# A hybrid encoder trunk: the 24 adaLN weight tiles of each layer move from the attention part to the branch part, into the ring of the weight stream

## The chip, the cores and the metric

The kernel runs on one core of a Trainium2 chip. The metric is device time of one execution in microseconds (us), the median of several runs. TensorE (PE) does the matmuls; VectorE (DVE), ScalarE (ACT) and GpSimd (POOL) do the rest; SyncE (SP) issues nearly all DMAs, in the order in which they are written.

## The reference, cut to what matters

Two requests of 256 tokens (512 columns in all) go through two layers of width 1024 with shared weights:

```python
mod = silu(c) @ w_mod + b_mod                    # (1024) x (1024, 6144), per request
sh1, sc1, gt1, sh2, sc2, gt2 = split(mod, 6)
h = rmsnorm(x) * (1 + sc1) + sh1
p = h @ w_in                                     # MLA, RG-LRU, DeltaNet inputs and three gates
o_mla, o_rg, o_gdn = mla(p), rglru(p), gdn(p)    # the three branches
m = sum_b sigmoid(gate_b) * (o_b @ w_branch[b])
x = x + gt1 * (m @ w_out)
h2 = rmsnorm(x) * (1 + sc2) + sh2
x = x + gt2 * convglu(h2)
```

In the RG-LRU each direction d has r = sigmoid(xb @ w_a + b_a), log_a = -8 * r * softplus(-lam), a = exp(log_a), and a factor sqrt(1 - exp(2 log_a)) on its input; then a scan over the tokens. The gated DeltaNet (GDN) has four heads, each a chain of small triangular solves and products.

## The kernel before, in words

Activations lie with channels on the 128 partitions and the 512 tokens on the free axis. Weights come as a stream of 128 x 128 units, eight to a chunk of 512 KB. `prefetch` (L375) loads a chunk into one of `NRAW = 3` buffers named `raw`, two chunks ahead of use; `split_chunk` (L382) splits it into a high part `wh` (ACT, L391) and a low part `wl` (DVE, L298), and each unit is then used by three matmuls of 512 columns (`mm3`).

The order of PE and SP is fixed by hand. `BRANCHES` (L33) lists the jobs of a layer: `in6` (first six input blocks), `uq`/`uk`/`uv` (up projections of MLA), `gate.b.d` and `br.b.d` (gate and branch product of branch b, output block d), `gq`/`gk`/`gv`/`z` (GDN), `x`/`g`/`b` (RG-LRU input, its gate, and the two products of one direction). Side work (attention, the GDN heads, the modulation) are generators that a `Driver` (L141) steps between the matmuls. The driver keeps a clock of its own, which adds an estimate for each matmul; a generator yields a wait of so many us (table `SLACK`) or an event, and is stepped when the clock has passed it. `drv.until(event)` steps what is due, and when nothing is, moves that clock ahead. The clock only decides where instructions stand in PE's and SP's order; on the chip an instruction waits for its data alone.

The modulation of a layer (`modulation`, L443, and `mod_gen`) multiplies silu(c) with tiles of w_mod: one tile of 512 KB is four products of fp32 (eight matmul instructions, `mod<-mraw,csil`). Here 24 tiles are in question, blocks 4 to 9, whose values (gt1, sh2, sc2) are first read in the output projection. Before the change they are spawned right after `in6` (L1091): pace 5.0 on the driver's clock, two buffers `mraw` of their own (`mla_raw`, L1051), each next load written behind the products of a tile. `close` (L1117), which frees MLA's memory, waits for `ev_mod`, their end. The job `uk.0` begins with `drv.until(ev_ckv)`, and `ev_ckv` is set to 152.5 us after the low-rank norm was written (`SLACK["low_rank_out"]`, set at L791), so all tiles that are left are written ahead of `uk.0`.

After `close`, the branch part runs until `close2`: GDN heads (`solve`, then `combine`, whose DMAs dl, Lb, dx and W go over SP), the RG-LRU, gates and branch products. Tiles of the RG-LRU and the gates share a tag `rt` with `RT = 8` buffers. In `rg_scan` the decay is scaled on DVE (L933) and then read by an exp and a tanh on ACT (L935, L936).

Of the kernel before, what the change touches and what calls it, by code (L numbers as in the profile page):

```python
# [8 lines left out]
F32 = mybir.dt.float32  # L9
# [3 lines left out]
AF = mybir.ActivationFunctionType  # L13
ALU = mybir.AluOpType
# [4 lines left out]
P = 128  # L19
# [7 lines left out]
UC = 8  # L27
# [5 lines left out]
BRANCHES = """  # L33
    in6 gate.0.0 uq.0 uq.1 gate.0.1 uq.2 uq.3 uq.4 uq.5 uk.0 uk.1 gq.0 uk.2 gk.0 uk.3 pad uv gv.0
    gate.0.2 gate.0.3 gate.0.4 gate.0.5 gate.0.6 gate.0.7 br.0.0 br.0.1 br.0.2 br.0.3 br.0.4 br.0.5
    br.0.6 br.0.7 close gq.1 gk.1 gv.1 x.0 x.1 b.0.0 g.0 b.0.1 g.1 b.1.0 x.2 b.1.1 g.2 x.3 b.2.0
    b.2.1 gq.2 gk.2 gv.2 g.3 b.3.0 b.3.1 gate.1.0 br.1.0 gate.1.1 br.1.1 gq.3 gate.1.2 gate.1.3
    br.1.2 z.0 gk.3 br.1.3 gate.2.0 gv.3 gate.2.1 gate.1.4 z.1 gate.2.2 gate.1.5 br.1.4 gate.1.6 z.2
    gate.1.7 gate.2.3 gate.2.4 gate.2.5 br.1.5 br.1.6 br.1.7 z.3 gate.2.6 mid gate.2.7 br.2.0 br.2.1
    br.2.2 br.2.3 br.2.4 br.2.5 br.2.6 br.2.7"""  # L40


def jobs():
# [17 lines left out]
SLACK = {  # L61
    "modev": 0.7, "att_s": 3.2, "att_t": 1.8, "att_e": 1.0, "low_rank": 11.8, "low_rank_out": 152.5, "mla": 0.2,
# [3 lines left out]
    "rg_all": 16.0, "ssq": 6.5, "kq": 8.0, "norm": 2.8, "normed": 17.0, "mod1": 5.0, "mod2": 8.0,  # L66
    "kd": 0.1, "start": 0.6, "diag2": 4.6, "cq": 2.1, "lr_diag": 5.3, "diag": 30.4}


# [165 lines left out]
def _body(es, tc, nc, xT, cT, wall, wmod, pvec, fng, cst, rope, xinit, yT, dbg):  # L235
    V, A, G = nc.vector, nc.scalar, nc.gpsimd
    drv = Driver()
# [4 lines left out]
    sp = es.enter_context(tc.tile_pool(name="small", bufs=1))  # L242
    xp = es.enter_context(tc.tile_pool(name="xm", bufs=8))
    hp = es.enter_context(tc.tile_pool(name="h", bufs=1))
    wp = es.enter_context(tc.tile_pool(name="w", bufs=2))
# [5 lines left out]

    def fill(pool, size):
        return pool.tile([P, size // 4], F32, name="fill", tag="fill", bufs=1)
    fill(sp, 160)


    cs = cp.tile([P, NCC], F32, name="cs")
# [42 lines left out]
    def stt(out, a, s, b, op0, op1):  # L300
        V.scalar_tensor_tensor(out, a, s, b, op0, op1)  # L301
# [11 lines left out]
    def aux_tile(shape=(P, T), name="aux"):  # L313
        return aux.tile(list(shape), F32, name=name, tag="aux")
# [51 lines left out]
    GS = (slice(0, S), slice(S, T), slice(0, T))  # L366


    NRAW = 3
    state = {"l": 0, "u": 0, "piece": None, "job": ""}  # L370

    loads, pieces = {}, {}
# [2 lines left out]
    def prefetch(at):  # L375
        if at not in loads:
            loads[at] = wp.tile([P, UC * P], F32, name="raw", tag="raw", bufs=NRAW)
            nc.sync.dma_start(loads[at], wall[at])
        return loads[at]
# [58 lines left out]
    def preload(l, blocks, tile_of):  # L438
        for i in range(4 * len(blocks)):
            loaded[l, 4 * blocks[0] + i] = tile_of(4 * blocks[0] + i)  # L440


    def modulation(l, groups, pace, tile_of, ahead):  # L443
        todo = [4 * g[0] + i for g in groups for i in range(4 * len(g))]

        def load():
            if todo:
                i = todo.pop(0)
                loaded[l, i] = tile_of(l, i)
        for _ in range(ahead):  # L450
            load()
        return mod_gen(l, groups, pace, load)
# [87 lines left out]
    def setup(l):  # L540
        def pcol(name):
            o, w = PV[name]
            return pv[:, l, o:o + w]
        d = {}
        t = sp.tile([P, 8], F32, name="p_sp", tag="p_sp", bufs=2)
        nl = sp.tile([P, 8], F32, name="p_nl", tag="p_nl", bufs=2)
        V.tensor_scalar(nl, pcol("rg_lam"), -1.0, None, ALU.mult)
        softplus(t, nl, 8)
        V.tensor_scalar(t, t, 4.0, None, ALU.mult)
        d["sp4"] = t  # L550
        t = sp.tile([P, 16], F32, name="p_hb", tag="p_hb", bufs=2)
        o, _ = PV["rg_b_a"]
        V.tensor_scalar(t, pv[:, l, o:o + 16], 0.5, None, ALU.mult)
        d["hb"] = t
        t = sp.tile([P, 1], F32, name="p_ng", tag="p_ng", bufs=2)
        V.tensor_scalar(t, pcol("gdn_norm_g"), 0.5, None, ALU.mult)
        d["ng"] = t
        t = sp.tile([P, 8], F32, name="p_ea", tag="p_ea", bufs=2)
        A.activation(t, pcol("a_log"), AF.Exp)
        V.tensor_scalar(t, t, -1.0, None, ALU.mult)  # L560
        d["nea"] = t
        prm[l] = d
# [100 lines left out]
    for k in range(8):  # L663
        t = xp.tile([P, T], F32, name="x", tag="x")
        nc.sync.dma_start(t, xT[:, k, :])
        xs.append(t)
    for b in range(4):
        preload(0, (b,), mraw)
        if b < NRAW:
            prefetch((0, b))  # L670
    later(stp)
    acc = stp.tile([P, T], F32, name="acc")
    for k in range(8):
        t = stp.tile([P, T], F32, name="sq", tag="t", bufs=4)
# [4 lines left out]
    ssq = aux_tile((P, 4), "ssq")  # L679
# [26 lines left out]
    for l in range(depth):  # L706
# [5 lines left out]
        pr = prm[l]  # L712
# [7 lines left out]
        mstack = ExitStack()  # L720
        mp = mstack.enter_context(tc.tile_pool(name="mla", bufs=1, side="right"))
        M2 = 10
        rstack = ExitStack()
        rp = rstack.enter_context(tc.tile_pool(name="mraw", bufs=1))
        gdn = GDN(nc, tc, locals())
        mixed = [None] * 8
        cq, ckv, o_mla = [], [], []
# [190 lines left out]
        def rg_scan(i, d):  # L918
            xc, xh, xl = xcs[i]
            if d == 0:  # L920
                drv.until(rev[i])
            zr = gemm([(xh, xl)])
            zi = gemm([(xh, xl)])
            c = d * 4 + i
            if d == 0:
                dirs.append(ap.tile([P, 2, T], F32, name="rs", tag="rs", bufs=RS))
            s = dirs[0][:, d, :]
            u = ap.tile([P, T], F32, name="ru", tag="rt", bufs=RT)
            a = ap.tile([P, T], F32, name="ra", tag="rt", bufs=RT)
            m = ap.tile([P, T], F32, name="rm", tag="rt", bufs=RT)  # L930
            A.activation(s, zr, AF.Tanh, bias=pr["hb"][:, c:c + 1], scale=0.5)
            A.activation(u, zi, AF.Tanh, bias=pr["hb"][:, 8 + c:9 + c], scale=0.5)
            V.tensor_scalar(s, s, 1.0, pr["sp4"][:, c:c + 1], ALU.add, ALU.mult)  # L933
            stt(u, u, 1.0, xc, ALU.add, ALU.mult)
            A.activation(a, s, AF.Exp, scale=-1.0)  # L935
            A.activation(s, s, AF.Tanh)  # L936
            A.activation(m, a, AF.Square)
            stt(s, m, 1.0, s, ALU.add, ALU.mult)
            f = 0 if d == 0 else S - 1
            V.memset(s[:, f::S], 1.0)  # L940
            V.memset(a[:, f::S], 0.0)
            dirs.append((u, a))
            if d == 0:
                return
            s2 = dirs.pop(0)
            A.activation(s2, s2, AF.Sqrt, bias=tiny, scale=0.0625)
            for d, (u, a) in enumerate(dirs):
                mul(u, u, s2[:, d, :])
                o = slice(None, None, -1 if d else 1)
                V.tensor_tensor_scan(s2[:, d, o], a[:, o], u[:, o], 0.0, ALU.mult, ALU.add)  # L950
            h0, h1 = s2[:, 0, :], s2[:, 1, :]
            dirs.clear()
            add(h0, h0, h1)
            mul(xc, h0, gls[i])
            debug(f"org{i}_{l}", xc)
            split(xc, xh, xl)
            o_rg.append((xh, xl))
            rev["all"] = drv.event()
            rev["all"].set(SLACK["rg_all"])
# [86 lines left out]
            uv.clear()  # L1046


        ev_mod = drv.event()

        def mla_raw(l, i):  # L1051
            raw = rp.tile([P, UC * P], F32, name="mraw", tag="mraw", bufs=2)
            nc.sync.dma_start(raw, wmod[l, i])
            return raw

        def beside(gen):
            yield from gen
            ev_mod.set(0.0)


        def next_raw(l, i):
# [13 lines left out]
        for job in JOBS:  # L1075
            k, *ix = job
            state["job"] = k
            if k == "in6":
# [9 lines left out]
                key_rope(misc)  # L1088
                ev_cq.set(SLACK["cq"])
                drv.spawn(low_rank())  # L1090
                drv.spawn(beside(modulation(l, ((4, 5, 6, 7), (8, 9)), SLACK["mod1"], mla_raw, 2)))  # L1091
            elif k in ("gq", "gk", "gv"):
                if k == "gq" and ix[0] >= 2:
                    drv.until(gdn.ev_free[ix[0] - 2])
# [22 lines left out]
            elif k == "close":  # L1117
                for t in range(8):
                    debug(f"K{t}_{l}", Kt[:, t, :])
                    debug(f"Q{t}_{l}", Qt[:, t, :])  # L1120
                drv.until(ev_mod)
                fill(mp, 1888)
                rstack.close()
                mstack.close()
                RT, RS = 8, 2
                ap = stack.enter_context(tc.tile_pool(name="rg", bufs=1))
                g2stack = ExitStack()
                gdn.g2 = g2stack.enter_context(tc.tile_pool(name="g2", bufs=1, side="right"))
                for hd in range(4):
                    drv.spawn(gdn.solve(hd))  # L1130
                gdn.xi = gdn.g2.tile([P, 8, 16], F32, name="xi", tag="xi")
                nc.sync.dma_start(gdn.xi, xinit)
            elif k == "x":
# [21 lines left out]
            elif k == "close2":  # L1155
                stack.close()
                rstack = ExitStack()
                rp = rstack.enter_context(tc.tile_pool(name="oraw", bufs=1))
# [11 lines left out]
            elif k == "out":  # L1170
                d, g = ix
# [23 lines left out]
            elif k == "down":  # L1195
                d, g = ix
# [7 lines left out]
                t = x1[d]  # L1204
                for e in ((0, 1) if g == 2 else (g,)):
                    c = GS[e]
# [536 lines left out]
```

## Time and profile before

| what | value |
|---|---|
| median of 3 runs | 2112.28 us (2110.99 to 2116.43) |
| profiled execution, its own time | 2115.39 us |
| its span, first to last instruction | 2113.6 us |
| PE busy | 1976.4 us, 94% |
| DVE / ACT / POOL busy | 1246.3 / 817.0 / 256.7 us |
| mean granted TensorE clock | 0.953 of 2.4 GHz |

Times in the profile are us from the first instruction. The engine named in front of an operation did it; "out<-in" names the tile written and the tile read; "[idle before <-releaser]" is the time that the engine stood idle ahead of it and what ended that.

### The profile page before, as it was taken

How to read it: one execution, taken by the hardware profiler on the slowest of the kernel's cores; microseconds unless marked ns; L12 is line 12 of the kernel's file. 1: busy time of each engine (PE TensorE's matmuls, PEld its weight loads, DVE VectorE, ACT ScalarE, POOL GpSimd, SP SyncE). 2: the span in 40 equal slices, each digit the busy share in tenths (PEclk: the TensorE clock that was granted, in tenths of full speed). 3: DMA queues.
4: the chain of work that ended last, by engine and by line, in shares of the span. 5: the costliest groups of instructions: out<-in, count | busy, mean ns of one | idle time of the engine just before them, and what ended most of it. 6: DMA issues, size and time to landing. Idle time of an engine off the chain costs nothing.

```text
span 2113.6 us, 29530 instructions
## 1 busy us (share of the span) xinstructions
PE 1976.4 (94%) x11563; PEld 1580.1 (75%) x11563; DVE 1246.3 (59%) x2338; ACT 817.0 (39%) x1275; POOL 256.7 (12%) x511
## 2 busy tenths in 40 slices
PE   9939998999999999999996699979999999999998
PEld 5717776788788788887874377768887878888887
DVE  5606578766366766653355175888553667666534
ACT  3404437533233444432242153565332335444322
POOL 1100036131300100000011000361421001000000
PEclk9959999999999999999998599989999999999999
DMA  8362132231426233353544412321322353232333
GB/s 299 134 202 67 55 92 64 68 83 52 111 86 214 80 100 93 97 179 110 191 126 140 161 60 72 90 65 51 96 72 78 115 185 93 97 100 92 99 99 110
DMA packets 141852, 231.45 MB, mean 110 GB/s; under 512 B 79760, under 2 KB 84240, under 8 KB 141712
## 3 DMA queue, kind: packets, MB, share of 16 engines
q1 hardware_dynamic: 136240, 221.95, 33.9%
q10 hardware_dynamic: 5472, 7.61, 1.1%
q8 instruction: 91, 1.49, 0.3%
q14 instruction: 49, 0.40, 0.1%
HBM read 221.66 MB, written 7.86 MB: 109 GB/s over the span
## 4 chain that ended last, share of the span: by engine, by line
PE 80%; DVE 7%; DMA 6%; ACT 2%; issue 2%; POOL 1%; SPq 1%; DVEq 0%; ACTq 0%; POOLq 0%
PE mm_up L220 23%; PE mm_down L220 11%; PE mm_gate L220 10%; PE mm_br L220 6%; DMA mraw<-in_wmod_dram 4%; PE mm_in L220 3%; PE mm_out L220 3%; PE mod L220 2%; PE mm_gk L220 2%; PE mm_gq L220 2%; PE mm_gv L220 2%; PE mm_g L220 1%; PE att_s L220 1%; PE gdn_rec L220 1%; PE mm_z L220 1%
## 5 line engine op out<-in xcount | busy, mean ns | idle before, releaser
L298 DVE TENSOR_TENSOR wl<-raw,wh 128x1024 fp32r<-128x1024 f32 x304 | 373.8, 1230 | 320.9 <-ACT wh L391 314.5
L391 ACT CAST wh<-raw 128x1024 fp32r<-128x1024 f32 x304 | 318.7, 1049 | 501.3 <-PE mm_down L220 130.5
L220 PE MATMUL mm_up<-hh,wh 128*128 128x512 f32 x704 | 275.6, 391 | 3.5 <-POOL hh L308 3.5
L220 PE MATMUL mm_up<-hl,wh 128*128 128x512 f32 x704 | 275.6, 391 | 0.0
L220 PE MATMUL mm_up<-hh,wl 128*128 128x512 f32 x704 | 275.1, 391 | 0.0
L301 DVE SCALAR_TENSOR_TENSOR cv<-mm_up,pv,cv 128x510 f32<-128x510 f32 x176 | 131.2, 748 | 61.3 <-ACT cv L569 58.0
L220 PE MATMUL mm_gate<-hh,wh 128*128 128x512 f32 x384 | 160.6, 418 | 0.0
L220 PEld LDWEIGHTS mm_up<-hh,wh 128*128 128x128 f32 x704 | 132.9, 189 | 31.7 <-POOL hh L308 3.9
L220 PEld LDWEIGHTS mm_up<-hl,wh 128*128 128x128 f32 x704 | 133.0, 189 | 27.9 <-DVE hl L298 0.4
L220 PEld LDWEIGHTS mm_up<-hh,wl 128*128 128x128 f32 x704 | 133.0, 189 | 27.5
L220 PE MATMUL mm_gate<-hl,wh 128*128 128x512 f32 x384 | 150.8, 393 | 0.0
L220 PE MATMUL mm_gate<-hh,wl 128*128 128x512 f32 x384 | 150.8, 393 | 0.0
L220 PE MATMUL mm_down<-ah,wh 128*128 128x512 f32 (+1 forms) x396 | 146.1, 369 | 0.0
L220 PE MATMUL mm_down<-ah,wl 128*128 128x512 f32 (+1 forms) x396 | 145.0, 366 | 0.6 <-DVE wl L298 0.6
L220 PE MATMUL mm_down<-al,wh 128*128 128x512 f32 (+1 forms) x396 | 144.9, 366 | 0.0
L220 PE MATMUL mod<-mraw,csil 128*32 128x256 f32 x512 | 56.3, 532 | 73.2 <-DMA mraw<-in_wmod_dram 73.0
L308 POOL TENSOR_SCALAR hh<-hn 128x256 fp32r<-128x256 f32 x64 | 34.0, 544 | 684.9 <-ACT hn L586 682.4
L569 ACT ACTIVATE cv<-mm_up,pv 128x512 f32<-128x512 f32 x88 | 68.5, 780 | 89.2 <-PE mm_up L220 89.2
L220 PEld LDWEIGHTS mod<-mraw,csil 128*32 128x32 f32 x512 | 12.3, 128 | 112.2 <-DMA mraw<-in_wmod_dram 102.3
L220 PEld LDWEIGHTS mm_down<-ah,wh 128*128 128x128 f32 x396 | 74.7, 189 | 15.0 <-issue 3.3
L220 PEld LDWEIGHTS mm_gate<-hh,wl 128*128 128x128 f32 x384 | 72.6, 189 | 16.0
L220 PEld LDWEIGHTS mm_down<-ah,wl 128*128 128x128 f32 x396 | 74.7, 189 | 13.0 <-DVE wl L298 0.8
(386 smaller groups left out, 3973.8 us busy)
## 6 DMA issues: line engine op xcount, KB each, us to landing
raw<-in_wall_dram SPq DMA_DIRECT2D x304, 512.0 KB, 3.6
mraw<-in_wmod_dram SPq DMA_DIRECT2D x64, 512.0 KB, 4.2
oraw<-in_wmod_dram SPq DMA_DIRECT2D x16, 512.0 KB, 7.1
hraw<-in_wmod_dram SPq DMA_DIRECT2D x32, 256.0 KB, 5.2
x<-in_xT_dram SPq DMA_DIRECT2D x8, 256.0 KB, 6.0
W<-dx SPq DMA_DIRECT2D x32, 64.0 KB, 2.3
xr<-in_xT_dram ACTq DMA_DIRECT2D x8, 256.0 KB, 3.3
xdram<-x ACTq DMA_DIRECT2D x16, 128.0 KB, 2.5
```

The source lines that it names most:

```text
L220: return self.pe.matmul(out, lhsT, rhs, **kw)
L298: (eng or V).tensor_tensor(out, a, b, ALU.subtract)
L301: V.scalar_tensor_tensor(out, a, s, b, op0, op1)
L308: G.tensor_scalar(hi, x, 1.0, 0.0, ALU.mult, ALU.add)
L391: A.copy(wh, raw)
L569: A.activation(dst, ps, AF.Identity, bias=bias, scale=w[lo])
```

## The change

The descriptor space of software DMAs is cut to 2 KB, which gives 14 KB per partition. They go to a fourth `raw` buffer (4 KB) and to `RT = 13`, five more `rt` tiles (10 KB). The two `mraw` buffers go; the 24 tiles of w_mod are spawned at `close`, at pace 8.0, one load ahead, from the ring of the `raw` buffers. Seven of the eight gates of branch 1 are written between the RG-LRU's products, ahead of `br.1.0`. The scale of the decay becomes scale and bias of the two ACT instructions.

```diff
-    gate.0.2 ... close gq.1 gk.1 gv.1 x.0 x.1 b.0.0 g.0 b.0.1 g.1 b.1.0 x.2 b.1.1 g.2 x.3 b.2.0
-    b.2.1 gq.2 gk.2 gv.2 g.3 b.3.0 b.3.1 gate.1.0 br.1.0 gate.1.1 br.1.1 gq.3 gate.1.2 gate.1.3
-    br.1.2 z.0 gk.3 br.1.3 gate.2.0 gv.3 gate.2.1 gate.1.4 z.1 gate.2.2 gate.1.5 br.1.4 gate.1.6 z.2
-    gate.1.7 gate.2.3 gate.2.4 gate.2.5 br.1.5 br.1.6 br.1.7 z.3 gate.2.6 mid gate.2.7 br.2.0 br.2.1
+    ... close gq.1 gk.1 gv.1 x.0 x.1 b.0.0 g.0 b.0.1 gate.1.0 g.1 b.1.0 x.2 b.1.1 gate.1.1
+    g.2 x.3 b.2.0 gate.1.2 b.2.1 gq.2 gk.2 gv.2 gate.1.3 g.3 b.3.0 gate.1.4 b.3.1 gate.1.5 gate.1.6
+    br.1.0 br.1.1 gq.3 br.1.2 z.0 gk.3 br.1.3 gate.2.0 gv.3 gate.2.1 br.1.4 z.1 gate.2.2 br.1.5
+    gate.1.7 z.2 br.1.6 gate.2.3 gate.2.4 br.1.7 gate.2.5 z.3 gate.2.6 mid gate.2.7 br.2.0 br.2.1
-    "mod1": 5.0
+    "mod1": 8.0
-    NRAW = 3
+    NRAW = 4
+        d["ns4"] = sp.tile([P, 8], F32, name="p_ns", tag="p_ns", bufs=2)
+        V.tensor_scalar(d["ns4"], t, -1.0, None, ALU.mult)
-            V.tensor_scalar(s, s, 1.0, pr["sp4"][:, c:c + 1], ALU.add, ALU.mult)
-            A.activation(a, s, AF.Exp, scale=-1.0)
-            A.activation(s, s, AF.Tanh)
+            p4, n4 = pr["sp4"][:, c:c + 1], pr["ns4"][:, c:c + 1]
+            A.activation(a, s, AF.Exp, bias=n4, scale=n4)
+            A.activation(s, s, AF.Tanh, bias=p4, scale=p4)
-        def mla_raw(l, i):
-            raw = rp.tile([P, UC * P], F32, name="mraw", tag="mraw", bufs=2)
+        def branch_raw(l, i):
+            raw = wp.tile([P, UC * P], F32, name="raw", tag="raw", bufs=NRAW)
             nc.sync.dma_start(raw, wmod[l, i])
-                drv.spawn(beside(modulation(l, ((4, 5, 6, 7), (8, 9)), SLACK["mod1"], mla_raw, 2)))
-                drv.until(ev_mod)
-                rstack.close()
-                RT, RS = 8, 2
+                RT, RS = 13, 2
+                drv.spawn(modulation(l, ((4, 5, 6, 7), (8, 9)), SLACK["mod1"], branch_raw, 1))
-    nc = _bacc.Bacc("TRN2", target_bir_lowering=False, num_devices=1)
+    nc = _bacc.Bacc("TRN2", target_bir_lowering=False, num_devices=1, dynamic_dma_scratch_size=2048)
```

## Rows read from the trace of the kernel before

**Rows 1.** Busy time by stretch; second row: layer 1; columns stand in the first line.
```profile
core 0: us, PE busy (x) PEld busy (x) DVE busy (x) ACT busy (x) POOL busy (x), PEclk, DMA share, GB/s
100.33:161.89 61.56, 24.09 (x178) 7.58 (x177) 3.89 (x11) 1.17 (x2) 0.00 (x0) 0.53 0.61 188
1140.60:1202.07 61.47, 24.22 (x178) 7.70 (x177) 3.89 (x11) 1.17 (x2) 0.00 (x0) 0.54 0.61 188
161.89:189.00 27.11, 26.43 (x110) 21.27 (x111) 14.40 (x21) 11.21 (x17) 0.00 (x0) 0.93 0.18 58
279.00:435.00 156.00, 141.29 (x1136) 115.08 (x1135) 130.62 (x255) 92.82 (x153) 59.67 (x111) 0.95 0.27 71
474.55:617.50 142.95, 139.09 (x1072) 115.35 (x1071) 71.19 (x134) 45.41 (x76) 26.13 (x64) 0.99 0.28 80
```

**Rows 2.** What PE waited for: us in total, times, longest.
```profile
PE mod L220 <- DMA mraw<-in_wmod_dram: 73.0, 32, 12.3
PE mm_x L220 <- DVE wl L298: 11.9, 2, 6.0
PE gdn_l L220 <- DMA W<-dx: 7.5, 2, 4.8
```

**Rows 3.** PE in order of time: start, us of one, operation, count, idle before.
```profile
56.15 0.95 PE L220 MATMUL mod<-cs,modev 128*128 128x2 f32 x8
...
81.57 0.39 PE L220 MATMUL mm_gate<-hl,wh 128*128 128x512 f32 x1
81.80 0.39 PE L220 MATMUL mm_gate<-hh,wl 128*128 128x512 f32 x1
82.11 0.64 PE L220 MATMUL mod<-mraw,csil 128*32 128x256 f32 x8
82.68 0.50 PE L220 MATMUL mm_gate<-hh,wh 128*128 128x512 f32 x1
...
118.60 1.08 PE L220 MATMUL mod<-mraw,csil 128*32 128x256 f32 x8 [2.60 <-DMA mraw<-in_wmod_dram]
```

**Rows 4.** DVE in order of time: the last operand of `uk`.
```profile
96.21 0.68 DVE L298 TENSOR_TENSOR cl<-lr,ch 128x512 fp32r<-128x512 f32 x1
```

**Rows 5.** SP in order of time: the rotary part's way into `Qt`.
```profile
106.27 0.80 SPq L814 DMA_DIRECT2D Qt<-drope  x2
```

**Rows 6.** DMA issues: count, KB each, median us to landing.
```profile
raw<-in_wall_dram SPq DMA_DIRECT2D x304, 512.0 KB, 3.6
mraw<-in_wmod_dram SPq DMA_DIRECT2D x64, 512.0 KB, 4.2
Qt<-drope SPq DMA_DIRECT2D x4, 256.0 KB, 5.1
```

**Rows 7.** Single lines, ns min/median/max: decay scale, exp, an ACTIVATE with two pointers.
```profile
L933 DVE TENSOR_SCALAR rs<-rs,p_sp x16: 470/486/719, 315.5 to 1461.3; 128x512 f32<-128x512 f32 x16
L935 ACT ACTIVATE ra<-rs x16: 612/632/647, 316.1 to 1461.9; 128x512 f32<-128x512 f32 x16
L569 ACT ACTIVATE xc<-mm_x,pv x8: 772/777/778, 306.3 to 1406.6; 128x512 f32<-128x512 f32 x8
```

**Rows 8.** What SP's queue waited for, 257 to 640 us.
```profile
SPq L1416 <- DVE cb L1412: 57.9, 4, 22.9
```

**Rows 9.** Landing times in the answers for tile Lb (with dl), then W.
```profile
DMA to landing us min/median/max: 1.8/2.2/4.6
...
DMA to landing us min/median/max: 2.0/2.3/3.8
```

**Rows 10.** DMA queues of the page: kind, packets, MB, share.
```profile
q1 hardware_dynamic: 136240, 221.95, 33.9%
q10 hardware_dynamic: 5472, 7.61, 1.1%
q8 instruction: 91, 1.49, 0.3%
q14 instruction: 49, 0.40, 0.1%
```

More of the change, by code (lines that the diff above doesn't have):

```diff
@@ L35 @@
     gate.0.2 gate.0.3 gate.0.4 gate.0.5 gate.0.6 gate.0.7 br.0.0 br.0.1 br.0.2 br.0.3 br.0.4 br.0.5
-    br.0.6 br.0.7 close gq.1 gk.1 gv.1 x.0 x.1 b.0.0 g.0 b.0.1 g.1 b.1.0 x.2 b.1.1 g.2 x.3 b.2.0
-    b.2.1 gq.2 gk.2 gv.2 g.3 b.3.0 b.3.1 gate.1.0 br.1.0 gate.1.1 br.1.1 gq.3 gate.1.2 gate.1.3
-    br.1.2 z.0 gk.3 br.1.3 gate.2.0 gv.3 gate.2.1 gate.1.4 z.1 gate.2.2 gate.1.5 br.1.4 gate.1.6 z.2
-    gate.1.7 gate.2.3 gate.2.4 gate.2.5 br.1.5 br.1.6 br.1.7 z.3 gate.2.6 mid gate.2.7 br.2.0 br.2.1
+    br.0.6 br.0.7 close gq.1 gk.1 gv.1 x.0 x.1 b.0.0 g.0 b.0.1 gate.1.0 g.1 b.1.0 x.2 b.1.1 gate.1.1
+    g.2 x.3 b.2.0 gate.1.2 b.2.1 gq.2 gk.2 gv.2 gate.1.3 g.3 b.3.0 gate.1.4 b.3.1 gate.1.5 gate.1.6
+    br.1.0 br.1.1 gq.3 br.1.2 z.0 gk.3 br.1.3 gate.2.0 gv.3 gate.2.1 br.1.4 z.1 gate.2.2 br.1.5
+    gate.1.7 z.2 br.1.6 gate.2.3 gate.2.4 br.1.7 gate.2.5 z.3 gate.2.6 mid gate.2.7 br.2.0 br.2.1
     br.2.2 br.2.3 br.2.4 br.2.5 br.2.6 br.2.7"""
@@ L65 @@
     1.8, "Y": 2.5, "v1": 3.6, "S": 0.8, "r": 2.9, "v2": 5.1, "on": 1.7, "o": 35.8, "rope": 1.5,
-    "rg_all": 16.0, "ssq": 6.5, "kq": 8.0, "norm": 2.8, "normed": 17.0, "mod1": 5.0, "mod2": 8.0,
+    "rg_all": 16.0, "ssq": 6.5, "kq": 8.0, "norm": 2.8, "normed": 17.0, "mod1": 8.0, "mod2": 8.0,
     "kd": 0.1, "start": 0.6, "diag2": 4.6, "cq": 2.1, "lr_diag": 5.3, "diag": 30.4}
@@ L253, in fill @@
         return pool.tile([P, size // 4], F32, name="fill", tag="fill", bufs=1)
-    fill(sp, 160)
+    fill(sp, 96)
     cs = cp.tile([P, NCC], F32, name="cs")
@@ L668, in _body @@
         preload(0, (b,), mraw)
-        if b < NRAW:
+        if b < 3:
             prefetch((0, b))
@@ L722, in _body @@
         M2 = 10
-        rstack = ExitStack()
-        rp = rstack.enter_context(tc.tile_pool(name="mraw", bufs=1))
         gdn = GDN(nc, tc, locals())
@@ L1046, in up @@
             uv.clear()
-        ev_mod = drv.event()
-        def mla_raw(l, i):
-            raw = rp.tile([P, UC * P], F32, name="mraw", tag="mraw", bufs=2)
+        def branch_raw(l, i):
+            raw = wp.tile([P, UC * P], F32, name="raw", tag="raw", bufs=NRAW)
             nc.sync.dma_start(raw, wmod[l, i])
             return raw
-        def beside(gen):
-            yield from gen
-            ev_mod.set(0.0)
         def next_raw(l, i):
```

## The prediction

> **What bounds the kernel now.** I read the page's busy times first: PE is busy 94% of the span, so time is won only where PE idles, runs at its lower clock, or does less. Next PE's waits in total: by far the longest is 73.0 us over 32 waits for w_mod tiles [rows 2]; the others together are small. Then the stretches where these waits lie [rows 1]: from 100.33 to 161.89 us, and again in layer 1 from 1140.60 to 1202.07, PE is busy 24 of 61.5 us, at a mean clock of 0.53, that is nearly all at the 1.2 GHz level, while DVE, ACT and POOL do next to nothing. PE's own order shows why: one tile of 512 KB feeds eight short instructions, then PE waits for the next ([rows 3], the row at 118.60 with 2.60 us idle). Nothing else is written between them, since the driver's clock is moved ahead by 152.5 us at `uk.0`. So each layer has a stretch in which one DMA-bound task runs alone and the other engines stand still. The branch part is different: PE is busy 141.3 of 156 us from 279 to 435 with DVE at 130.6, and 139.1 of 143 us from `gk.3` to `br.2.0` [rows 1].
>
> **The change part by part, for one layer, at layer 0's times.**
>
> *The MLA part.* The stretch of 61.5 us goes: after the last `uq` matmul comes `uk.0` at once. Of the 24 tiles 20 lay in it and 4 among gates and `uq` before it. Such a tile at the 2.4 GHz level costs: matmuls follow each other by 0.227 us (81.57, 81.80), so without the tile the next would have started at 82.03; it starts at 82.68 and is 0.11 us longer than its neighbours, 0.76 us in all [rows 3]. Four of them: 3.0 us. And 161.89 to 189 us runs at 0.93 [rows 1], because PE comes out of the waits at 1.2 GHz; without them I take 1.0: 7% of 27.1 = 1.9 us. Sum: 61.5 + 3.0 + 1.9 = 66.4 us less.
>
> What is late next there? `uk.0` needs ckv, whose last operand ends at 96.89 [rows 4], 3.4 us ahead of 100.33. Attention needs the rotary half of Qt, issued at 106.27, the second of two done issuing at 107.07, landing 5.1 us later, 112.2 [rows 5, 6]; it was first used some 25 us behind `uk.0`, hence now near 125. The next weight chunk is written behind those two transfers, so it lands at 107.1 + 3.6 = 110.7; PE's order asks for its split 16 units behind `uk.0`, 16 x 0.68 = 10.9 us, at 111.3. That is close, but the split chunk is used another six units (4.1 us) later. I cost this at nothing; if the cover fails it is 2 to 3 us.
>
> *The tiles in the branch part.* All 24 now cost 24 x 0.76 = 18.2 us of PE, and the two selections behind them (eight small matmuls, 0.95 us each, the first row of [rows 3]) 1.9: 20.1 us more. Beside other work on PE nothing hides, so this is on the path unless it falls into PE's idle time.
>
> *Waits for these tiles.* A load is written behind the products of the tile before; on the driver's clock the tile is due 8.0 us later, its transfer takes 4.2 [rows 6]. So 3.8 us are left for SP to be late. SP is late when a transfer ahead in its queue waits: dl for cb, 57.9 us over four heads, mostly because SP is early, not late [rows 8]. Behind a waiting w_mod load the weight chunks queue too, but they are asked for two chunks (10.9 us) ahead. Below, no wait: 0; above, every tile as in the old stretch, 73.0 us over 48 tiles, 1.5 us each, 36 us a layer. I take 3 us, near the lower end, since 24 x 8.0 = 192 us fits nearly twice into a branch part of some 340 us and the driver seldom has to jump there.
>
> *Gates between the products.* The gates only change places, 24 matmuls x 0.227 = 5.4 us each, so their sum is nought; what counts is idle time. From 279 to 435 PE idles 14.7 us, and 5% of lost clock on 156 us is 7.8 more: 22.5 us to be had [rows 1]. DVE is the cause, 84% busy; the longest wait of these, 6.0 us once per layer, is `mm_x` for a `wl` that stood behind the RG-LRU's work in DVE's queue [rows 2]. Each gate in between gives DVE 5.4 us in which nothing new comes to it, and the decay's scale leaves it: 8 x 0.486 = 3.9 us [rows 7]. Bounds: 0 and 22.5 back. I take 73% of it, 16.4 us: 5 gates and some 15 tiles in a stretch whose DVE load then falls from 84% to about 71% (126.7 us in 156 + 27 + 11.4 - 16.4 = 178).
>
> *The end of the branch part.* The same move takes three gates (16.3 us) from between `gk.3` and `br.2.0`, and there head 3's chain of solves runs: now 143 us with 3.9 us idle, one wait being the chain itself, `gdn_l` for W, 7.5 us in both layers [rows 1, 2]. With less to lay beside it the chain shows. Bounds: all 16.3 us come back as idle time, or none. I take 9, a little over half: the last part of the chain is written at the pace of the driver's table and runs quicker when PE does nothing else, and two or three tiles still fall there.
>
> *The other edits.* Exp and tanh get scale and bias from tiles. An ACTIVATE with two such pointers takes 0.777 us, L935 without them 0.632 [rows 7]: 16 x 0.145 = 2.3 us more on ACT a layer, at 92.8 of 156 us not the bound; 0. RT = 13 must hold the gates' seven tiles beside the RG-LRU's own; where it doesn't, a gate's tanh waits for a scan: 0 to 5 us, inside the term above. The fourth `raw` buffer is what the w_mod tile occupies, so the weight stream keeps three: 0. The smaller descriptor space: no queue of the page carries software descriptors [rows 10], 0. One DVE instruction of 8 columns more per layer: 0.
>
> *Sum.* Branch part: 20.1 + 3 - 16.4 + 9 = +15.7. Layer: -66.4 + 15.7 = -50.7. Two layers: -101.4. The profiled execution took 2115.4 us (2113.6 of span and 1.8 around it), hence 2014.0; it stands 3.1 us over the median of the runs, so for the median 2112.3 - 101.4 = 2010.9, say 2011.
>
> **A rule that speaks against it.** The transfers of the solves are small and share SP's queue with the loads; the longest landing among dl and Lb is 4.6 us against a median of 2.2, for W 3.8 against 2.3 [rows 9]. So some already wait behind others, by up to 2.4 and 1.5 us. The Trainium skill, DMA: Bandwidth & Descriptors, section Queues, rings and completion order, says that on one DMA engine the descriptors of a queue are taken in ring order. By that rule a 512 KB load put ahead of a small transfer delays it, and 24 more loads per layer do so more often. The rows bear it out by their maxima alone. As a mechanism of this kernel it is the second rival.
>
> **The rivals.** (1) *The waits only move (slower).* The tile's load is written one ahead; where the driver jumps or SP is held up, PE waits the whole landing, 4.2 us, and falls to 1.2 GHz again. If every tile did: 24 x 4.2 = 100.8 us a layer, net -66.4 + 12.7 + 100.8 = +47.1, and 2112 + 94 = 2206. It decides from (66.4 - 12.7) / 24 = 2.2 us per tile on. For it: DVE holds up SP over cb by up to 22.9 us [rows 8]. Against: in the old part the four tiles that stood among other matmuls cost no wait at all (82.11 in [rows 3]), at a pace of 5.0, though with two loads ahead. Chance 0.04. (2) *Solve transfers queue behind loads.* dl and Lb 2.4 us each, dx the same by estimate, W 1.5: 8.7 us a head; shown on PE by all four heads 34.8 us a layer, 2011 + 70 = 2081; it decides from PE's waits for W being over 30 us in all. Against: heads 0 to 2 have other work beside them. Chance 0.06. (3) *Nothing is won back in the branch part*: no idle recovered, all 16.3 us of the end shown, 10 us of waits: 20.1 + 16.3 + 10 = +46.4, net -20 a layer, 2072. For it: DVE's work hardly shrinks. Chance 0.14. (4) *All is won back*: 20.1 - 22.5 = -2.4, net -68.8, 1975. For it: the tiles and gates are just the work without DVE that PE lacked. Chance 0.24. (5) *The stretch stays*, since something else holds `uk.0` or attention: within 2100 and 2125; the row of ckv speaks against it. Chance 0.03.
>
> **How the numbers follow.** My sum holds with 0.49, between 1990 and 2035. Range 1976 to 2052: it takes in (4) nearly whole and part of the way to (3), and leaves out (1), (5) and the farther ends of (2) and (3). Within 0.3% (6 us, what a measurement of this kernel can tell): 0.02 from (5); slower 0.05, from (1) and (5); faster 0.93.
>
> **What would show it.** Right: no stretch in the MLA part with PE's clock near 0.5; `uk.0` less than 1 us behind the last `uq`; attention starting some 63 to 67 us earlier; products of w_mod at some 0.76 us a tile, lying among the branch part's matmuls, with waits for their tiles under 10 us in all; the branch part longer by 5 to 30 us per layer; PE idle from 279 to 435's work cut to a third; a wait of several us in head 3's chain. Wrong: waits for w_mod tiles over 50 us in all; PE's waits for ckv, Qt or `wl` in the MLA part; waits for W over 30 us; or the wait of `mm_x` for `wl` standing as before.

## The result and the profile after

The changed kernel takes 2019.88 us (median of 4 runs, 2017.35 to 2026.03) against 2114.36 for the kernel before in the same series: ratio 0.956, 95% interval 0.953 to 0.959, 94.5 us faster. A second series gave 2019.63 us and 0.954 (0.953 to 0.956). The profiled execution took 2019.3 us, its span 2017.5; PE is busy 1949.8 us of it (97%), at a mean clock of 0.986. The forecast was 2011, its range 1976 to 2052. The span fell by 96.1 us where the sum said 101.4; this is 5.3 of the 9.0 us by which the forecast (2010.9 before rounding) was short. The rest is that the profiled execution of before stood 3.1 us above its median and that of after 0.6 us below its own.

The busy times by stretch, in the columns of [rows 1]. The first two rows lie in the MLA part of layers 0 and 1: from within `uk.0`, whose first matmuls stand at 97.33 and 1091.06, to attention's second group of scores; the next two are the branch parts of both layers; the last two are layer 0's branch part split at `gk.3`.

```profile
98.97:130.61 31.64, 26.11 (x102) 20.32 (x101) 16.76 (x22) 11.11 (x16) 0.00 (x0) 0.89 0.45 133
1092.00:1121.97 29.97, 25.00 (x105) 19.81 (x104) 16.06 (x21) 11.19 (x16) 0.00 (x0) 0.94 0.47 141
220.74:573.55 352.81, 335.13 (x2645) 264.48 (x2645) 220.46 (x436) 152.27 (x242) 105.17 (x212) 0.98 0.38 110
1212.10:1565.03 352.93, 335.21 (x2645) 264.42 (x2645) 220.47 (x436) 152.28 (x242) 105.18 (x212) 0.99 0.39 110
220.74:439.40 218.66, 208.00 (x1670) 160.61 (x1670) 155.36 (x303) 110.94 (x172) 76.49 (x149) 0.98 0.44 123
439.40:573.55 134.15, 127.14 (x976) 103.87 (x975) 65.10 (x134) 41.34 (x71) 28.68 (x64) 0.97 0.30 87
```

The stretch of 61.5 us at a clock of 0.53 is gone. These are attention's first matmuls in layer 0, before:

```profile
186.64 1.03 PE L220 MATMUL att_s<-Kt,Qt 96*128 96x256 f32 x4
```

and after, 58.2 us earlier:

```profile
128.45 1.03 PE L220 MATMUL att_s<-Kt,Qt 96*128 96x256 f32 x4
```

The branch part before, in layer 0 whole and up to `gk.3`, then whole in layer 1:

```profile
278.90:617.50 338.60, 320.04 (x2438) 263.00 (x2437) 224.72 (x434) 147.65 (x240) 104.32 (x212) 0.96 0.29 77
278.90:474.55 195.65, 180.94 (x1368) 147.65 (x1367) 153.53 (x300) 102.24 (x165) 78.19 (x148) 0.95 0.29 75
1319.41:1661.24 341.83, 321.39 (x2437) 264.08 (x2437) 224.18 (x434) 147.61 (x240) 105.02 (x212) 0.96 0.28 76
```

In layer 0 it now has 207 more PE instructions and lasts 352.81 us instead of 338.60. PE idles 17.7 us in it, against 18.6 before.

What PE waits for in all (compare [rows 2]):

```profile
PE gdn_l L220 <- DMA W<-dx: 15.5, 6, 6.2
PE mm_uk L220 <- ACT wh L391: 9.6, 2, 4.8
PE spread L220 <- DVE onx L301: 4.6, 2, 2.3
PE ssq L220 <- DVE osq L295: 4.0, 2, 2.0
```

No wait for a w_mod tile is left, and the two waits of 6.0 us of `mm_x` for `wl` are gone. There are new ones. The second row lies in the MLA part, where the forecast had put nothing; the first, the longest of which rose from 4.8 to 6.2 us, and the last two lie in the branch part.

A tile among branch matmuls, in PE's order:

```profile
303.04 0.39 PE L220 MATMUL mm_gate<-hh,wl 128*128 128x512 f32 x1
303.35 0.64 PE L220 MATMUL mod<-raw,csil 128*32 128x256 f32 x8
303.92 0.50 PE L220 MATMUL mm_gate<-hh,wh 128*128 128x512 f32 x1
```

Without it the next matmul would have followed at 303.04 + 0.23 = 303.27; it starts at 303.92 and is 0.11 us longer: 0.76 us a tile, as at the old place [rows 3].

### The profile page after: what moved, and what is told of

The parts are those of the page before. It is cut to its first block, busy times and chain, and to the rows that moved or that the text cites. A ratio compares the mean times of both kernels' runs of the same rounds, so it can differ in the third digit from the quotient of the medians.

```text
span 2017.5 us, 29521 instructions
## 1 busy us (share of the span) xinstructions
PE 1949.8 (97%) x11563; PEld 1564.2 (78%) x11563; DVE 1235.5 (61%) x2324; ACT 823.9 (41%) x1275; POOL 258.0 (13%) x511
## 4 chain that ended last, share of the span: by engine, by line
PE 82%; DVE 5%; POOL 4%; DMA 4%; issue 2%; ACT 2%; SPq 2%; POOLq 0%; ACTq 0%; DVEq 0%
PE mm_up L220 24%; PE mm_down L220 12%; PE mm_gate L220 10%; PE mm_br L220 6%; PE mm_in L220 3%; PE mm_out L220 3%; PE mm_gk L220 2%; PE mod L220 2%; PE mm_gq L220 2%; POOL xt L292 2%; PE mm_gv L220 2%; POOL X L298 2%; PE att_s L220 1%; PE gdn_rec L220 1%; PE gdn_l L220 1%
## 5 line engine op out<-in xcount | busy, mean ns | idle before, releaser
L220 PEld LDWEIGHTS mm_gate<-hh,wh 128*128 128x128 f32 x384 | 73.0, 190 | 22.2 <-issue 7.4
L220 PEld LDWEIGHTS mm_gate<-hh,wl 128*128 128x128 f32 x384 | 72.7, 189 | 16.4
L220 PEld LDWEIGHTS mm_down<-al,wh 128*128 128x128 f32 x396 | 74.7, 189 | 11.9
```

The source lines that it names most:

```text
L220: return self.pe.matmul(out, lhsT, rhs, **kw)
```

## The experiments

Ratios are to runs of the kernel before on the same chip, with 95% intervals; the changed kernel stands at 2019.6 us and 0.954.

**One constant of the old kernel.** No memory is moved: only the wait behind the low-rank norm is shortened.

```diff
-    "low_rank_out": 152.5
+    "low_rank_out": 5.0
```

> The kernel before with one number changed: the driver's wait ahead of uk.0 from 152.5 to 5.0 us. The w_mod tiles stay beside MLA, with their two buffers and pace 5.0. My theory (the DMA-bound stretch was made by that number; beside attention the tiles cost only their products): 61.5 + 1.9 - 20 x 0.76 = 48 us a layer less, 96 in all, about 2018 us, as fast as the change itself. Rival, the MLA part can't take them (PE is busy 68 of 68 us there, SP and the psum banks are shared with attention): waits for tiles of 1 us or more each, or the same stretch again at close, 2040 us or more.

Measured: 2023.95 us, 0.956 (0.955 to 0.958). This one number gives the gain of the whole change, within some 4 us. With two buffers of their own, the tiles spread among the matmuls of the MLA part; this is the stretch from 97 us to attention's second group of scores (the first is at 125.28):

```profile
97.00:127.59 30.59, 29.63 (x155) 21.09 (x153) 18.83 (x26) 13.25 (x25) 0.00 (x0) 1.00 0.61 200
```

PE is busy 29.6 of 30.6 us at full clock. So the cause of the old stretch was that the hand-written order put all tiles ahead of `uk.0`; their buffers and transfers were not too slow. By these two times the whole change is worth hardly more than the constant; the next run shows what hides the difference.

**The old order of gates**, with all else of the change.

```diff
-    ... b.0.1 gate.1.0 g.1 b.1.0 x.2 b.1.1 gate.1.1 g.2 x.3 b.2.0 gate.1.2 ... gate.1.6 br.1.0
+    ... b.0.1 g.1 b.1.0 x.2 b.1.1 g.2 x.3 b.2.0 ... b.3.1 gate.1.0 br.1.0 gate.1.1 br.1.1 ...
```

> The changed kernel with the job order of before; the w_mod tiles stay in the branch part. My theory (gates between the RG-LRU's products win back some 16 us of idle time and lower clock a layer and lose some 9 at the end of the branch part): 7 us a layer slower, 14 in all, about 2034 us, PE idle before gk.3 up again and the long wait of mm_x for wl back. Rival A, the tiles alone fill PE's idle time: within 3 us of the changed kernel. Rival B, the end of the branch part loses more than the products win: 5 to 20 us faster than the changed kernel.

Measured: 2010.81 us (2000.27 to 2015.03), 0.949 (0.947 to 0.951). The five runs lie 15 us apart, but the intervals of this kernel and of the changed one don't meet: the reorder costs some 9 us. It is spent in the branch parts, which take 349.1 and 348.1 us here instead of 352.8 and 352.9. Layer 0's branch part whole and up to `gk.3`, then layer 1's:

```profile
220.55:569.64 349.09, 338.93 (x2646) 267.13 (x2645) 220.39 (x436) 151.55 (x242) 106.18 (x212) 0.97 0.38 111
220.55:423.86 203.31, 195.48 (x1528) 150.13 (x1526) 150.73 (x298) 105.60 (x166) 78.74 (x148) 0.96 0.43 122
1211.09:1559.15 348.06, 336.19 (x2645) 264.54 (x2645) 220.90 (x436) 150.96 (x242) 106.33 (x212) 0.98 0.38 111
```

PE's waits for W are down from 15.5 us, and those of `mm_x` for `wl` have not come back:

```profile
PE gdn_l L220 <- DMA W<-dx: 9.9, 5, 3.3
PE mm_x L220 <- DVE wl L298: 1.1, 2, 0.7
```

So the tiles alone fill the idle time among the products: up to `gk.3` PE idles 7.8 us here, 10.7 with the change's order and 14.7 before.

This kernel and the one with the constant have the same order of gates, and this one, with the tiles in the branch part and all else of the change, is 13 us better (0.949 against 0.956, intervals apart). Beside MLA, where PE is busy throughout, 20 tiles and the selections made the way from `uk.0` to `gq.1` 15.8 us longer in layer 0 (132.7 against 116.9), near the 17.1 of their products. In the branch part all 24, 20.1 us by the prediction's count, made it only 10.5 us longer. No run takes the freed memory (`RT` = 13, the fourth `raw` buffer) by itself.

**No loads.** All tiles of a layer read one loaded tile.

```diff
-            raw = wp.tile([P, UC * P], F32, name="raw", tag="raw", bufs=NRAW)
-            nc.sync.dma_start(raw, wmod[l, i])
-            return raw
+            if (l, "one") not in loads:
+                ...
+            return loads[l, "one"]
```

> The changed kernel with 23 of the 24 w_mod loads of each layer's branch part left out: all products read the first tile, so the modulation's values are not the reference's; the products on PE stay. My theory (the loads cost nothing on PE directly, but lengthen the small transfers of the solves, Lb from 2.2 to 3.9 us and W from 2.3 to 3.0): landings back to about 2.2 and 2.3, the waits for W fall from 15.5 to about 8 us, 5 to 8 us faster, about 2013 us. Rival A, the loads are quite free: within 3 us. Rival B, most of what the branch part gained in length, 11 to 14 us a layer, is due to loads: 20 us or more faster.

Measured: 2021.39 us, 0.955 (0.953 to 0.956), with PE's waits as they were:

```profile
PE gdn_l L220 <- DMA W<-dx: 16.5, 6, 6.4
```

The loads cost nothing in the branch part that these times can show, so they are not why PE waits for W. The median landing of `Lb` did rise with the change, from 2.2 [rows 9] to 3.9 us, and is 3.1 without the loads, so 0.8 of the 1.7 us go with them. That is the direction of the rule of the Trainium skill, DMA: Bandwidth & Descriptors, section Queues, rings and completion order, that was weighed in the prediction; it shows in the landing and not in the time.

**The wait for `wh`: one chunk load ahead of the rotary transfers.** The gap of 4.8 us per layer stands in `uk`, at 118.28.

```diff
                 dr = dp.tile([P, 2, T], F32, name="drope", tag="drope")
+                prefetch((l, (state["u"] + AHEAD) // UC + 2))
                 nc.sync.dma_start(dr, x)
```

> The changed kernel with one weight chunk's load (the one that uk.3 waits for, 4.78 us in each layer) written ahead of the three transfers of the rotary part. My theory (the load stood in SP's queue behind these transfers and shared the DMA engines with them): the waits of mm_uk for wh go, 2 x 4.8 us, and with them 1 to 3 us of lower clock a layer: 11 to 16 us faster than the changed kernel, about 2007 us. Rival, the cast or its slot is late for another reason: the wait stays, within 3 us of the changed kernel. Rival 2, Qt comes late instead: a wait of att_s takes the place of it, within 5 us.

Measured: 2020.62 us, 0.955 (0.954 to 0.957). The wait moved one chunk on:

```profile
PE mm_uv L220 <- ACT wh L391: 6.9, 2, 3.5
```

**Two chunk loads ahead of them.**

```diff
+                c = (state["u"] + AHEAD) // UC + 2
+                prefetch((l, c))
+                prefetch((l, c + 1))
                 nc.sync.dma_start(dr, x)
```

> The changed kernel with two weight chunks' loads written ahead of the rotary part's transfers (with one the wait passed to the next chunk, 3.5 us at uv). My theory (a load behind the two Qt transfers lands some 11 us after its issue; two chunks cover that): no wait for wh in the MLA part, uk.0 to att_s 27 us at most instead of 33, 8 to 14 us faster than the changed kernel, about 2009 us. Rival, the wait passes on again or the loads delay the rotary part and with it att_s: within 4 us of the changed kernel.

Measured: 2004.84 us (2003.95 to 2007.39), 0.947 (0.946 to 0.949): 15 us less, no wait for `wh`. What changed shows in ACT's order. In the changed kernel:

```profile
113.54 0.69 ACT L569 ACTIVATE gc<-mm_gk,pv 128x512 f32<-128x512 f32 x1 [2.31 <-PE mm_gk L220]
116.67 0.63 ACT L1299 ACTIVATE kq<-gc 128x512 f32<-128x512 f32 x1 [2.44 <-DVE gc L301]
117.20 1.98 ACT L391 CAST wh<-raw 128x1024 fp32r<-128x1024 f32 x2
```

With two chunk loads ahead:

```profile
106.36 1.05 ACT L391 CAST wh<-raw 128x1024 fp32r<-128x1024 f32 x1 [0.44 <-PE mm_uk L220]
...
111.80 1.05 ACT L391 CAST wh<-raw 128x1024 fp32r<-128x1024 f32 x1 [1.74 <-PE mm_gk L220]
112.76 0.68 ACT L569 ACTIVATE gc<-mm_gk,pv 128x512 f32<-128x512 f32 x1
...
117.75 0.63 ACT L1302 ACTIVATE kq<-gc 128x512 f32<-128x512 f32 x1
```

The order of ACT, unlike PE's and SP's, is not written by hand. In the changed kernel the two casts stand behind the conv steps of head 0's `gk` (`gc`, then `kq`), in the other ahead of them. In the changed kernel the load that PE waits for was issued here on SP, and its landing is the line below it:

```profile
105.62 0.37 SPq L378 DMA_DIRECT2D raw<-in_wall_dram  x1
...
DMA to landing us min/median/max: 6.6/6.6/6.6
```

It was there at 105.6 + 6.6 = 112.2. The 11 us in the expectation are no landing: they reach to the start of the cast. ACT was idle for 2.31 us up to 113.54 and for 2.44 up to 116.67. PE stopped at 113.50. A cast at 112.2 would have ended at 113.3, in time for PE's first matmul. So by the rows most of the wait is the place in ACT's order; about 1 us of it would have been left by the landing, since `wl` takes DVE 1.2 us more. PE came out of the gap at its lower level:

```profile
113.11 0.39 PE L220 MATMUL mm_gk<-hh,wl 128*128 128x512 f32 x1
118.28 0.80 PE L220 MATMUL mm_uk<-ch,wh 128*128 128x512 f32 x1 [4.78 <-ACT wh L391]
118.88 0.63 PE L220 MATMUL mm_uk<-cl,wh 128*128 128x512 f32 x1
```

That the order was planned so because the load was expected late, behind the rotary transfers, fits both experiments but is an inference.

**The rotary transfers from ACT's queue.** In the changed kernel the load of the chunk for `uk.3` stands behind these two on SP.

```diff
-                    nc.sync.dma_start(Qt[64 + 16 * e:80 + 16 * e], ...)
+                    nc.scalar.dma_start(Qt[64 + 16 * e:80 + 16 * e], ...)
```

> The change with the two rotary transfers to Qt issued from ACT's queue instead of SP's; everything else as in the change. [...] Theory A, order within SP's queue: the load's descriptors stand behind 512 KB of the two transfers in the same rings; then from another queue the load lands in 4 to 7 us, PE's wait in uk for wh (9.6 us in two) is gone or under 3 us, and the time falls by 5 to 14 us to 2006 to 2015. [...] A third: ACT reaches the issue late or stalls on it, and attention starts later, 2022 us and more, with a wait of the scores for Qt.

Measured: 2012.55 us (2004.36 to 2013.18), 0.950 (0.948 to 0.952), the wait for `wh` gone; in the profiled execution, the fastest (2004.36), attention starts at 119.77. This is what theory A gave, but it doesn't decide for it: here too one cast moved ahead in ACT's order (106.25, where the changed kernel has none from 102.43 to 117.20), and the chunk loads were issued at 100.2, before the transfers at 102.8. The transfers themselves, issued now behind loads already under way on the other queue, land in 9.5 to 11.6 us, against 4.3 to 6.0 in the changed kernel. Whether a load behind the transfers is delayed by the queue's order or by the traffic itself stays open.

**Decay scale back on DVE.**

```diff
+            V.tensor_scalar(s, s, 1.0, pr["sp4"][:, c:c + 1], ALU.add, ALU.mult)
-            A.activation(a, s, AF.Exp, bias=n4, scale=n4)
-            A.activation(s, s, AF.Tanh, bias=p4, scale=p4)
+            A.activation(a, s, AF.Exp, scale=-1.0)
+            A.activation(s, s, AF.Tanh)
```

> The change with the decay's scale back on DVE: 16 instructions of 0.486 us a layer return to DVE, and the exp and tanh on ACT lose their two pointers, 0.145 us each by my working. My prediction costed the edit at nothing by itself: 2019.6 us, within 3 us either way. Rival: DVE's 84% load from 279 to 435 us was what PE waited for, so the 8 x 0.486 = 3.9 us of a layer show in whole: 2027 us, with longer waits of the products for wl or of matmuls for DVE. Second rival: the chain of ACT through exp and tanh is what br.1.0 waits for, and the time falls by 1 to 3 us.

Measured: 2021.34 us, 0.955 (0.953 to 0.957); no difference. (The scale is 8 instructions a layer, not 16: [rows 7] counts both layers.) The exp with two pointers takes 0.806 us in the changed kernel (0.632 in [rows 7]), so 0.17 us more, where I had taken 0.145:

```profile
L935 ACT ACTIVATE ra<-rs,p_ns x16: 801/806/828, 258.1 to 1387.1; 128x512 f32<-128x512 f32 x16
```

**Three gates back behind `gk.3`**, four stay among the products.

```diff
-    b.2.1 gq.2 gk.2 gv.2 gate.1.3 g.3 b.3.0 gate.1.4 b.3.1 gate.1.5 gate.1.6 br.1.0 ...
+    b.2.1 gq.2 gk.2 gv.2 gate.1.3 g.3 b.3.0 b.3.1 br.1.0 ... gate.1.4 z.1 gate.2.2 gate.1.5 br.1.4 gate.1.6 br.1.5
```

> The changed kernel with gates 1.4 to 1.6 written behind gk.3 again, where they stood before; gates 1.0 to 1.3 stay between the products. Theory A (the old order was 9 us faster because the end of the branch part lacked these three gates): 5 to 10 us faster than the changed kernel, about 2011 us, the waits of ssq and of gdn_l for W smaller. Theory B (the gates between the products cost it): as the changed kernel, within 3 us.

Measured: 2022.56 us, 0.956 (0.954 to 0.957). The waits for W fall from 15.5 to 5.6 us, and another takes their place:

```profile
PE mm_br L220 <- ACT xch L310: 14.3, 2, 7.9
PE mm_uk L220 <- ACT wh L391: 9.6, 2, 4.8
PE gdn_l L220 <- DMA W<-dx: 5.6, 4, 2.2
```

Nothing now stands between the last product of the RG-LRU and `br.1.0`, which needs its output; the run doesn't tell what the three gates alone are worth.

**The old order with two chunk loads ahead.**

> The changed kernel with the job order of before and two chunks' loads written ahead of the rotary part's transfers. If both findings hold and lie in different stretches, they add: 9 + 8 to 14 us, 1997 to 2003 us. If the two are one (the loads' place decides both), as the old order alone, about 2011 us.

Measured: 1997.79 us (1989.62 to 2002.07), 0.943 (0.941 to 0.945). The two gains add up nearly: 13 us against the old order, 7 against the two chunks alone, 21.8 against the changed kernel where 9 and 15 make 24.

**A slower pace of the tiles**, on that kernel.

```diff
-    "mod1": 8.0
+    "mod1": 12.0
```

> The old order with two chunk loads ahead (1997.8 us), and the pace of the w_mod tiles 12.0 instead of 8.0: the 24 tiles of a layer spread over 288 us of the driver's clock instead of 192, so that some six to eight more of them stand behind gk.3 beside the chain of solves of head 3. If the tiles are worth more as cover there than in the stretch before, the time falls by 2 to 6 us and PE's idle time from gk.3 to br.2.0 with it. Rival: the stretch ahead of gk.3 needs them as much (its idle time grows by what the other loses), 1998 us, within 3 us. Third: the last tiles come too late and close2 waits for the selections, 2000 us and more, with a wait of PE for mod or for a w_mod tile at the end of the branch part.

Measured: 1996.66 us, 0.943 (0.941 to 0.945): no difference, the first rival. The waits for W fall to 3.5 us, but with fewer tiles among the products `mm_x` waits for `wl` again:

```profile
PE mm_x L220 <- DVE wl L298: 6.9, 2, 3.6
```

**Two gates among the products, two right ahead of `br.1.0`, three behind `gk.3`**, and two chunk loads ahead.

```diff
-    g.2 x.3 b.2.0 gate.1.2 b.2.1 gq.2 gk.2 gv.2 gate.1.3 g.3 b.3.0 gate.1.4 b.3.1 gate.1.5 gate.1.6
+    g.2 x.3 b.2.0 b.2.1 gq.2 gk.2 gv.2 g.3 b.3.0 b.3.1 gate.1.2 gate.1.3
     br.1.0 br.1.1 gq.3 br.1.2 z.0 gk.3 br.1.3 gate.2.0 gv.3 gate.2.1
-    br.1.4 z.1 gate.2.2 br.1.5
+    gate.1.4 z.1 gate.2.2 gate.1.5 br.1.4 gate.1.6 br.1.5
```

> The change with two chunk loads ahead of the rotary transfers (2004.8 us in the run before), and of the seven gates of branch 1 only 1.0 and 1.1 stand between the RG-LRU's products; 1.2 and 1.3 stand right ahead of br.1.0, and 1.4 to 1.6 behind gk.3, as in the old order. It parts two places at which the new order can cost its 7 to 9 us. Theory A, the end of the branch part lacks cover (three gates were taken from behind gk.3): with those three back the time comes to that of the old order with two chunks, 1997.8 us, within 3 us, the waits of PE for W fall from 15.5 to about 10 us or less, and from gk.3 to br.2.0 PE idles some 4 us less per layer. Theory B, the cost lies in the gates that stand between the products: they delay the products, the scan and so br.1.0; two of them still stand there, so about two fifths of the cost stay, 2000 to 2002 us. Theory C, neither: 2003 to 2006 us, or slower with a new wait for the RG-LRU's output ahead of br.1.0, as with three gates moved back in an earlier run (14.3 us in two waits).

Measured: 1981.88 us (1976.60 to 1983.66), 0.936 (0.933 to 0.938), the best of all; none of the three theories reached so far (1997.8 at the lowest). The branch part of layer 0, first in this kernel, then with the old order and two chunks, then with the change's order and two chunks:

```profile
212.82:551.80 338.98, 331.48 (x2645) 261.78 (x2645) 220.17 (x436) 152.31 (x242) 103.77 (x212) 0.99 0.40 114
```

```profile
212.75:561.26 348.51, 339.02 (x2645) 266.74 (x2645) 220.95 (x436) 151.38 (x242) 106.93 (x212) 0.97 0.39 111
```

```profile
211.87:565.97 354.10, 337.81 (x2646) 266.59 (x2645) 220.34 (x436) 152.32 (x242) 106.89 (x212) 0.98 0.39 109
```

The same work in three orders. PE idles 7.5, 9.5 and 16.3 us; the rest of the difference, 7.5 and 6.3 us, is PE's longer busy time on the same matmuls, at a mean clock of 0.97 and 0.98 against 0.99. The last two profiled executions were the slowest of their five, 4.3 and 2.6 us over the median, so the rows overstate the difference a little. The waits of this kernel's branch part are short:

```profile
PE gdn_l L220 <- DMA W<-dx: 6.2, 4, 2.5
PE mm_gv L220 <- DVE wl L298: 4.3, 2, 2.1
```

The waits of `ssq` and `spread` at the branch part's end are gone, and none has come at `br.1.0`. So the cost lay in neither place alone: with four gates among the products and none ahead of `br.1.0` the wait moved there, with two ahead of it and three behind `gk.3` it is in neither place. Whether the two gates left among the products matter is not shown. Why it undercuts the old order by so much is shown only as idle time and clock; the two differ in four gates and in where `br.1.5` to `br.1.7` stand, and I did not take these apart.

## Why the prediction held, and where it did not

The mechanism was right: the time came from the stretch in which one task ran alone, and the tiles cost in the branch part about what their matmuls cost, less some recovery. By its steps, per layer, where the MLA part is read from when attention starts, and layer 1's terms are set against the end of layer 0's branch part:

| step | predicted | layer 0 | layer 1 |
|---|---|---|---|
| MLA part | -66.4 | -58.2 | -63.4 |
| branch part | +15.7 | +14.2 | +11.1 |
| sum | -50.7 | -44.0 | -52.3 |

**What was mis-sized: the chunk behind the rotary transfers**, "I cost this at nothing; if the cover fails it is 2 to 3 us". The cover failed, and cost 4.8 us of waiting and the matmuls at the lower level after it. So attention came 58.2 us earlier in layer 0, not the 63 to 67 named as a sign. With two chunk loads ahead it starts at 119.79, 66.9 us earlier than before, of which 1.3 lie at the kernel's start (the first `mm_in` at 23.8 instead of 25.1); layer 1's term is -65.8. The MLA term without this failure is as predicted. My landing was 1.5 us short (110.7 against 112.2), and only because two errors met: the load was issued 1.5 us earlier than I took it and needed 6.6 us instead of 3.6. The larger fault was to reason from landing times alone: the cast also has a place in ACT's queue, and that place changed with SP's order. The rows of ACT before could not show it, but the working took ACT's order as fixed without saying so. The text on the kernel before says that on the chip an instruction waits for its data alone; by these rows it also waits for those ahead of it on its engine.

**Waits for the tiles**: 0 measured, 3 predicted. That drops the first rival: a pace of 8.0 against a median landing of 3.6 us was cover enough.

**Gates between the products, and the end of the branch part.** The sum came out near in layer 0, the parts did not: 3 us too much for waits and 5.4 too much at the end made up for 6.9 us too much won back among the products. That the sum fits is luck. Up to `gk.3` layer 0's branch part grew from 195.65 to 218.66 us. Of the 208 added products 168 stand there, 81% of 20.1 = 16.2 us, and with the three gates of 16.3 us that makes 32.5; it grew by 23.0, so 9.5 us were won back, not 16.4. Behind `gk.3` it shrank from 142.95 to 134.15, 8.8 us, where 16.3 left and 3.9 came: the end showed 3.6 us instead of 9. Both are good to about 1 us, as 64 small products of the GDN also moved ahead of `gk.3`. A cut of PE's idle time to a third was a sign; it fell from 14.7 to 10.7 us. The old-order run corrects the reasoning behind these terms. I credited the gates with giving DVE air; the tiles alone did that (1.1 us of `mm_x` waits left), and DVE's relief by the decay's scale is not to be seen in the time. The gates taken from further back left gaps there: a wait of 6.2 us for W in head 2 (3.3 at most with the old order) and one of 2.0 us of `ssq` at the end of head 3's chain (1.1). The wait of `spread` behind it, 2.3 us, stands with the old order too, so it has another cause. This is how the first of them looks; the z matmuls behind it run at the 1.2 GHz level until 435.3, and the mean granted clock from 427 to 437 is 0.66:

```profile
431.13 1.08 PE L220 MATMUL gdn_l<-W,B 32*32 32x32 f32 x64 [6.17 <-DMA W<-dx]
...
433.15 0.63 PE L220 MATMUL mm_z<-hh,wl 128*128 128x512 f32 x1
...
435.54 0.40 PE L220 MATMUL mm_z<-hh,wl 128*128 128x512 f32 x1
```

**The rivals.** Solve transfers queueing behind loads: refuted, waits for W stay at 16.5 us with nearly no loads. Nothing won back: no, 14 and 11 us of growth against 46. All won back: not in this change, but the last run's branch part is 338.98 us against 338.60 before (340.75 against 341.83 in layer 1), with all tiles in it, so nearly all was within reach of another order. The stretch stays: no.

**The edits costed at nothing.** The decay's scale stayed so within the noise (+1.7 us with it back on DVE). `RT` = 13, the fourth buffer and the smaller descriptor space were not run by themselves. The loads of the tiles cost nothing either (+1.8 us without them).

## What to carry to other kernels

When one task runs alone with the clock down, look first for the line that puts it there: here a constant of 152.5 in a hand-written order gave nearly the gain of the whole change. What the move is worth beyond it came out only with the gates where they had been (13 us). Work moved as filler must be counted at the place it leaves as well as where it goes: here the long chains did best with something independent right ahead of the matmul that waits for them. When the order of one engine's queue is changed and another engine's order is planned from it, read that other order again, since a tile that has landed is of no use while its cast stands behind a waiting instruction.

## What the runs showed of the chip

A gap of 4.8 to 6.2 us on PE costs more than its length: behind each, matmuls of 0.39 us took 0.63 for several us. Over a branch part PE's busy time differed by 6 to 8 us between orders of the same 2645 instructions, the last run's being the shortest. Two transfers of 256 KB from ACT's queue, with loads of 512 KB under way from SP's, landed in 9.5 to 11.6 us, against 4.3 to 6.0 from SP's queue ahead of the loads.
